# Fixed places for the side work on TensorE and VectorE in a one-core transformer layer

## The chip, the core and the metric

The kernel runs on one core of one Trainium2 chip. The metric is device time in microseconds (us): lower is better. Every time below comes from repeated runs of the kernel or from one profiled execution of it.

## The reference

One layer works on 256 latent tokens and 256 context tokens of width 2048, all in float32. Only the latent stream is returned.

```python
mod_x = split((silu(c) @ w_mod + b_mod), 6)          # shift, scale, gate; shift, scale, gate
h  = rms_norm(x, g_mix) * (1 + mod_x[1]) + mod_x[0]  # and the same for the context tokens
qa, ka, va, qb, kb, vb, rb, lrf, lrb, gate_a, gate_b = split(h @ w_in)
qa, ka = rope(rms_norm(qa)), rope(rms_norm(ka))
o_attn = windowed_attention(qa, ka, va, cka, cva, sink)        # 16 query heads, 4 key heads
o_gla  = latent_gla(qb, kb, vb, gf, gb, context states)        # 4 heads, forward and backward
y_att  = o_attn @ w_attn_o
y_gla  = (rms_norm(o_gla) * silu(rb)) @ w_gla_o
x = x + mod_x[2] * ((sigmoid(gate_a) * y_att + sigmoid(gate_b) * y_gla) @ w_out)
h2 = rms_norm(x, g_ffn) * (1 + mod_x[4]) + mod_x[3]            # the second norm
u  = conv3(h2 @ w_up) ; a, g = split(u)
x = x + mod_x[5] * ((silu(a) * g) @ w_down)
```

## The kernel before

**Products.** Every operand of a large matrix product is written as a sum of a high and a low part in a reduced float32 form, and a product is three matmuls: high by high, low by high, high by low. Weights come in chunks of 256 rows by 512 columns (512 KB). A chunk is loaded by SyncE's DMA queue into one of seven `raw` tiles, ScalarE copies its high part to `whi` (L61) and VectorE subtracts to get the low part `wlo` (L62); there are three pairs of those. `proj_nat` (L165) multiplies a chunk with two token tiles (twelve matmuls of 512 columns: eight with `whi`, L176 and L177, then four with `wlo`, L181) or with four token tiles (24). `proj_T` (L185) makes transposed outputs, and `proj_pair` (L210) the up projection of the FFN, where one matmul takes the high and low part of `h2` side by side (L219, and L223 for the low weights).

**Side work.** At the head of each chunk `tick()` (L133) emits other work between the products: entries put off with `defer(n, ...)`, steps of one generator "beside" (the GLA of a head in `gla_A`, L509, or an attention group in `attend`, L757), and background steps at a rate in `bg_rate`. The background steps are `mod_latent` (L260): the latent tokens' modulation vector `silu(c) @ w_mod` is summed on VectorE, a raw chunk of `w_mod` at a time, by `macc` (two instructions to a chunk, L282 and L284); a finished part goes through a VectorE transpose and sum (`mtr` L288, `mrs` L290) and a small matmul (`pcl`, L294). These raw chunks go through the same seven `raw` tiles and the same queue as the weights.

**What sets the order.** Loads keep the order in which the program writes them (`load`, L66, chains them). On TensorE, VectorE and ScalarE a scheduler at build time sorts the instructions by its own estimates of when they are ready; on the chip each engine then runs its list in that order, and an instruction that waits holds all that stand behind it. Nothing in the program ties a matmul of the side work to a place between the products, nor a `macc` to a place between the `wlo`.

**Stages,** in the order of time: the first norm and the modulation; context and latent projections with the GLA beside them (to about 520 us), keys `KA` and values `VA` of the attention, the attention groups, the `RB` gate of the GLA output (to about 850 us), then the merge: `w_attn_o`, the two gates and `w_gla_o` in turn for four blocks of 512 columns (`mg_evac`, L873, adds the branches into `m` and puts off the transposes `to_T`, L831), `w_out` (to 1285 us), the second norm, the up projection in two halves with the down projection after each, and the store.

**Around the second norm.** `wo_evac` (L893) multiplies by the gate, adds to `x1`, squares on ScalarE, and puts off four transposes (`ptx1`, L903). After the last block come the sum of squares (L914), `rms_scale` (L325), `token_rows` (L339: two scaled identities `dg`, L344, two products `pr`, L345, and a copy `rrow`, L347), and for each of 16 row blocks `affine_split` (L392: VectorE L394, ScalarE L395, VectorE L396).

**Other places that are touched.** `with_gla` (L657) runs `gla_A` at 1.5 steps to a chunk; inside, the cross terms `kf` and `kg` (L610, L611) feed the products `pa` (L617). `gla_o` (L623) emits a head's output products. `ka_evac` (L723) normalises and rotates the keys (`norm_rope`, L700) and puts off their transposes `ptk` (L729). `rb_evac` (L839) makes `sr` (L844) and puts off its transposes. `dn_evac` (L975) is the end of the down projection.

## Time and profile before

| | |
|---|---|
| three runs | 2039.68, 2039.70, 2042.13 us (median 2039.7) |
| profiled execution | 2039.47 us, span 2037.7 us, mean granted TensorE clock 0.991 |
| TensorE busy | 1979.4 us, 97% |
| VectorE busy | 1430.0 us, 70% |
| ScalarE busy | 960.7 us, 47% |
| weight chunks split | 568, `whi` 1059 ns and `wlo` 1226 ns each |
| `macc` on raw `w_mod` | 240, 751 ns each |

The span is what the profile shows; the execution's own time is 1.8 us more. In a row of the timeline stand the start, the time from the first start to the last end, the engine, the line, the operation, the output and inputs, the size, how many instructions of the kind follow one another, and in brackets how long the engine had been idle before and what ended that. In a row of a window stand the stretch, its length, the busy time of TensorE, of its weight loads, of VectorE, ScalarE and GpSimd, then the granted TensorE clock (1.00 is full, 0.50 half), the share of the DMA engines and the rate. The row of a wait says which engine and line waited for what: us in total, times, the longest.

### The profile page before, as it was taken

What the parts mean: (1) busy time and instruction counts of PE and PEld (TensorE: products, weight loads), DVE (VectorE), ACT (ScalarE), POOL (GpSimd) and SP (SyncE); (2) the same over time, 40 slices, a digit from 0 to 9 for tenths busy, and PEclk for the clock granted to TensorE, in tenths of its full rate; (3) what the DMA queues carried; (4) which work ended last, traced back from release to release, by engine and by line L of the source; (5) the groups of instructions that cost most, each with busy time, mean ns of one, the idle gap of its engine ahead of it and who ended that gap; (6) DMA issues with size and microseconds to landing.
All of it is one profiled execution on the core that took longest, in us unless ns stands there. A gap on an engine that the chain in (4) does not pass through costs nothing.

```text
span 2037.7 us, 27395 instructions
## 1 busy us (share of the span) xinstructions
PE 1979.4 (97%) x10384; PEld 1647.3 (81%) x10384; DVE 1430.0 (70%) x2237; ACT 960.7 (47%) x1394; POOL 38.9 (2%) x62
## 2 busy tenths in 40 slices
PE   6999999999999999999999999899999999999998
PEld 4778888888787777787778888788888888888887
DVE  4657577887758888877775455788887555667754
ACT  4323464553345656444334444565555434556532
POOL 0001000001000000000000000000000000000000
PEclk8999999999999999999999999899999999999999
DMA  9977223345544456788886665577776656555563
GB/s 350 364 259 224 91 77 93 93 135 192 172 146 129 124 184 206 263 271 272 273 269 220 237 207 187 193 248 251 261 245 207 212 193 193 188 187 187 193 211 111
DMA packets 214340, 413.54 MB, mean 203 GB/s; under 512 B 12548, under 2 KB 21092, under 8 KB 213184
## 3 DMA queue, kind: packets, MB, share of 16 engines
q1 hardware_dynamic: 212320, 406.89, 60.5%
q0 software_dynamic: 1360, 4.74, 0.8%
q8 instruction: 81, 1.33, 0.3%
q14 instruction: 51, 0.42, 0.1%
q10 hardware_dynamic: 528, 0.17, 0.0%
HBM read 409.63 MB, written 2.11 MB: 202 GB/s over the span
## 4 chain that ended last, share of the span: by engine, by line
PE 78%; DVE 10%; DMA 8%; ACT 2%; issue 2%; DVEq 0%; POOL 0%; ACTq 0%; SPq 0%
PE acc L176 13%; PE acc L177 13%; PE acc L181 13%; PE acc L219 8%; PE accs L219 8%; DMA raw<-in_w_mod 8%; PE acc L223 4%; PE accs L223 4%; PE acc L203 3%; DVE wlo L62 3%; DVE macc L284 3%; PE acc L206 2%; PE pm L245 1%; PE pa L552 1%; ACT whi L61 1%
## 5 line engine op out<-in xcount | busy, mean ns | idle before, releaser
L61 ACT ACTIVATE whi<-raw 128x1024 fp32r<-128x1024 f32 x568 | 600.9, 1059 | 784.7 <-PE acc L177 500.7
L62 DVE TENSOR_TENSOR wlo<-raw,whi 128x1024 fp32r<-128x1024 f32 x568 | 694.1, 1226 | 335.4 <-ACT whi L61 302.6
L284 DVE SCALAR_TENSOR_TENSOR macc<-raw,ccol,macc 128x512 f32<-128x512 f32 x240 | 180.3, 751 | 110.5 <-DMA raw<-in_w_mod 107.0
L219 PE MATMUL acc<-h,whi 128*128 128x512 f32 x704 | 178.6, 396 | 2.2 <-DVE h L396 2.2
L219 PE MATMUL accs<-h,whi 128*128 128x512 f32 x704 | 176.3, 392 | 0.0
L219 PEld LDWEIGHTS acc<-h,whi 128*128 128x128 f32 x704 | 127.8, 191 | 25.6 <-DVE h L396 2.5
L219 PEld LDWEIGHTS accs<-h,whi 128*128 128x128 f32 x704 | 126.6, 189 | 22.6
L176 PE MATMUL acc<-whi,h00hi 128*128 128x512 f32 x352 | 141.2, 401 | 1.5 <-DVE kb L412 0.6
L176 PE MATMUL acc<-whi,h01hi 128*128 128x512 f32 x352 | 139.8, 397 | 0.0
L177 PE MATMUL acc<-whi,h00lo 128*128 128x512 f32 x352 | 139.8, 397 | 0.0
L177 PE MATMUL acc<-whi,h01lo 128*128 128x512 f32 x352 | 137.7, 391 | 0.0
L177 PE MATMUL acc<-whi,al 128*128 128x512 f32 x352 | 137.1, 389 | 0.0
L176 PE MATMUL acc<-whi,ah 128*128 128x512 f32 x352 | 137.0, 389 | 0.0
L223 PEld LDWEIGHTS acc<-h,wlo 128*128 128x128 f32 x704 | 97.0, 192 | 7.1
L223 PEld LDWEIGHTS accs<-h,wlo 128*128 128x128 f32 x704 | 96.0, 190 | 6.9
L223 PE MATMUL acc<-h,wlo 128*128 128x256 f32 x704 | 99.1, 284 | 0.0
L181 PE MATMUL acc<-wlo,h00hi 128*128 128x512 f32 x352 | 98.0, 394 | 0.2 <-DVE wlo L62 0.2
L223 PE MATMUL accs<-h,wlo 128*128 128x256 f32 x704 | 98.2, 282 | 0.0
L181 PE MATMUL acc<-wlo,h01hi 128*128 128x512 f32 x352 | 97.0, 393 | 0.0
L181 PE MATMUL acc<-wlo,ah 128*128 128x512 f32 x352 | 94.4, 389 | 0.0
L176 PEld LDWEIGHTS acc<-whi,h00hi 128*128 128x128 f32 x352 | 66.9, 190 | 15.6 <-ACT kb L410 0.7
L181 PEld LDWEIGHTS acc<-wlo,h00hi 128*128 128x128 f32 x352 | 65.8, 189 | 14.4 <-DVE wlo L62 1.0
(375 smaller groups left out, 3461.5 us busy)
## 6 DMA issues: line engine op xcount, KB each, us to landing
raw<-in_w_in SPq DMA_DIRECT2D x208, 512.0 KB, 4.1
raw<-in_w_up SPq DMA_DIRECT2D x176, 512.0 KB, 3.6
raw<-in_w_mod SPq DMA_DIRECT2D x128, 512.0 KB, 4.0
raw<-in_w_down SPq DMA_DIRECT2D x88, 512.0 KB, 3.7
mraw<-in_w_mod SPq DMA_DIRECT2D x32, 1024.0 KB, 11.9
raw<-in_w_attn_o SPq DMA_DIRECT2D x32, 512.0 KB, 4.5
raw<-in_w_gla_o SPq DMA_DIRECT2D x32, 512.0 KB, 4.7
raw<-in_w_out SPq DMA_DIRECT2D x32, 512.0 KB, 3.6
```

Source lines behind the costliest of these rows:

```text
L61: S.activation(hi, src, AF.Copy)
L62: V.tensor_tensor(lo, src, hi.bitcast(F32), op=ALU.subtract)
L176: PE.matmul(banks[i], ahi, hi[:, k, :], start=(kt == kts[0]), stop=False)
L177: PE.matmul(banks[i], alo, hi[:, k, :], start=False, stop=False)
L181: PE.matmul(banks[i], l(kt)[0], lo[:, k, :], start=False, stop=(kt == kts[-1]))
L203: PE.matmul(o, w_, ahi, start=(kt == kts[0] and b == 0 and part == 0), stop=(kt == kts[-1] and part == 1), skip_group_check=True)
L206: PE.matmul(o, w_, alo, start=False, stop=False, skip_group_check=True)
L219: PE.matmul(banks[f], hi[:, k, f * P:(f + 1) * P], pair(k0 + k), start=(k0 + k == kts[0]), stop=False, skip_group_check=True)
L223: PE.matmul(banks[f][:, 0:T], lo[:, k, f * P:(f + 1) * P], pair(k0 + k)[:, 0, :], start=False, stop=(k0 + k == kts[-1]), skip_group_check= ...
L245: PE.matmul(a[0][q:q + 32, :], cS[:, kt, :], raw[:, k, :], start=(kt < 4), stop=(kt >= 12))
L284: V.scalar_tensor_tensor(a[0], raw[:, k, :], ccol[:, kt:kt + 1], a[0], op0=ALU.mult, op1=ALU.add)
L552: PE.matmul(pa[:, t, :], k2[:, dt, t * P:(t + 1) * P], q2[:, dt, tq * P:(tq + 1) * P], start=(dt == 0), stop=(dt == 1))
```

## The change

The kernel computes the same. It adds 34 matmuls on TensorE; the other engines run the same instructions in another order.

- `mm` notes the last matmul of the projections; `tick` takes it as a pin, and `mm_b` and `turn_b` (now used by all side work on TensorE) make a side matmul stand behind the product that was emitted last ahead of its tick. A dependency without a semaphore ties only the order on the engine.
- A `macc` step stands behind the last `wlo` that was emitted before it.
- `tick` runs all entries that are due, not only those at the head of the list.
- `gla_A` runs at 1.65 steps to a chunk and yields once more ahead of `pa` from `kf`. The outputs of the last head are put off by a tick.
- The transposes of the keys come after 2, 3, 4, 5 ticks instead of 1, 1, 2, 2, and their `y` tile moves to another set of four buffers; those of `rb` and of the merge after 3 and 4 instead of 1 and 2.
- `by_tile`: in the last block of `w_out` and of the last `w_down`, the last chunk does all six products of the first token tile, then those of the second.
- Around the second norm: the scale is made ready early; TensorE's order is the last transposes, 20 transposes of the identity (`pd1`), the two `pr`, 14 more (`pd2`), the first up product; the first `wlo` of the up projection stands behind the last add to `x1`, the others behind the second pair of `h2` that their chunk needs; the `h2` instructions have a fixed order, and the `macc` of the last modulation part come after them all.
- In the last block of the store, the first tile's add stands ahead of the second tile's multiply.

```diff
 
     def split(hi, lo, src):
         S.activation(hi, src, AF.Copy)
-        V.tensor_tensor(lo, src, hi.bitcast(F32), op=ALU.subtract)
+        return V.tensor_tensor(lo, src, hi.bitcast(F32), op=ALU.subtract).ins
+
+    def in_order(*ins):
+
+        for a, b in zip(ins, ins[1:]):
+            tc.add_manual_dep(b, a.name, mybir.DependencyInfo(
+                mybir.DependencyClass.NoSync, mybir.DependencyReason.DATA), reason="order")
+
+    last, pin = [None], [None]
+
+    def mm(*a, **k):
+
+        r = PE.matmul(*a, **k)
+        last[0] = r.ins
+        return r
+
+    def after(i):
+
+        if pin[0] is not None:
+            tc.add_manual_dep(i.ins, pin[0].name, mybir.DependencyInfo(
+                mybir.DependencyClass.NoSync, mybir.DependencyReason.DATA), reason="place among the products")
+        return i
+
+    def mm_b(*a, **k):
+        return after(PE.matmul(*a, **k))
+
+    def turn_b(*a):
+        return after(PE.transpose(*a))
...
 
     def tick():
 
+        pin[0] = last[0]
         for e in later:
             e[0] -= 1
-        while later and later[0][0] < 0:
-            later.pop(0)[1]()
+        due = [e for e in later if e[0] < 0]
+        later[:] = [e for e in later if e[0] >= 0]
+        for e in due:
+            e[1]()
         if beside:
             beside[2] += beside[1]
             while beside[2] >= 1.0:
...
         while bg_rate[1] >= 1.0 and bg_steps:
             bg_rate[1] -= 1.0
             bg_steps.pop(0)()
+        pin[0] = None
 
...
+    hold, last_lo = [], [None]
...
             hi = wh.tile([P, 2, 512], F32R, name="whi", tag="whi")
             lo = wh.tile([P, 2, 512], F32R, name="wlo", tag="wlo")
             n = src.shape[0] // P
-            split(hi[:, 0:n, :], lo[:, 0:n, :], raw[:, 0:n, :])
+            i = split(hi[:, 0:n, :], lo[:, 0:n, :], raw[:, 0:n, :])
+            if hold:
+                in_order(hold.pop(0), i)
+            last_lo[0] = i
         return hi, lo
 
-    def proj_nat(w, r0, c0, kts, lhs, evac):
+    def proj_nat(w, r0, c0, kts, lhs, evac, by_tile=False):
+
 
...
+            if by_tile and k0 + nk > kts[-1]:
+                for i in range(len(lhs)):
+                    part0(i)
+                    part1(i)
+                    if i:
+                        in_order(end, mms[-4])
+                    end = mms[-1]
+            else:
+                for part in (part0, part1):
+                    for i in range(len(lhs)):
+                        part(i)
...
+    behind = []
...
-                    PE.matmul(banks[f], hi[:, k, f * P:(f + 1) * P], pair(k0 + k),
-                              start=(k0 + k == kts[0]), stop=False, skip_group_check=True)
+                    i = mm(banks[f], hi[:, k, f * P:(f + 1) * P], pair(k0 + k),
+                                  start=(k0 + k == kts[0]), stop=False, skip_group_check=True).ins
+                    if behind:
+                        in_order(behind.pop(), i)
...
-    def mod_latent(parts, put=lambda fn: defer(3, fn)):
+    def mod_latent(parts, put=lambda fn: defer(3, fn), begin=None):
...
                 if kt == 0:
-                    V.tensor_scalar(a[0], raw[:, 0, :], ccol[:, 0:1], None, op0=ALU.mult)
+                    i0 = V.tensor_scalar(a[0], raw[:, 0, :], ccol[:, 0:1], None, op0=ALU.mult).ins
+                    if begin is not None:
+                        in_order(begin, i0)
                 else:
-                    V.scalar_tensor_tensor(a[0], raw[:, k, :], ccol[:, kt:kt + 1], a[0],
-                                           op0=ALU.mult, op1=ALU.add)
+                    i0 = V.scalar_tensor_tensor(a[0], raw[:, k, :], ccol[:, kt:kt + 1], a[0],
+                                                op0=ALU.mult, op1=ALU.add).ins
+                if k == 0:
+                    in_order(last_lo[0], i0)
...
-                    PE.matmul(pc, sel[:, 0:32], rs, start=True, stop=True)
+                    mm_b(pc, sel[:, 0:32], rs, start=True, stop=True)
...
         yield
+        yield
         pa = bank("pa", (P, 2, T), side=True)
         for t in range(2):
             for i, (kk, qq) in enumerate(((kf, q2), (kg, q3))):
                 for dt in range(2):
-                    PE.matmul(pa[:, t, :], kk[:, dt, t * P:(t + 1) * P], qq[:, dt, :],
+                    mm_b(pa[:, t, :], kk[:, dt, t * P:(t + 1) * P], qq[:, dt, :],
                               start=(i == 0 and dt == 0), stop=(i == 1 and dt == 1))
...
-        beside[:] = [gla_A(h, kb, qbt, res), 1.5, 0.0]
+        beside[:] = [gla_A(h, kb, qbt, res), 1.65, 0.0]
...
-        gla_o(h, a, *v)
+        if h < 3:
+            gla_o(h, a, *v)
+    defer(1, lambda: gla_o(3, a, *v))
...
-        z = norm_rope(b, rk if i < 2 else None, i % 2)
+        z = norm_rope(b, rk if i < 2 else None, i % 2, "fa")
...
-                PE.transpose(pt[:, h, :], z[:, h, :], ident)
+                turn_b(pt[:, h, :], z[:, h, :], ident)
...
-        defer(1 + i // 2, turn)
+        defer(2 + i, turn)
...
-            defer(1 + t, lambda: to_T(s_, gh, gl, j, t))
+            defer(3 + t, lambda: to_T(s_, gh, gl, j, t))
...
-            defer(1 + t, lambda: to_T(a2[t], mh, ml, j, t))
+            defer(3 + t, lambda: to_T(a2[t], mh, ml, j, t))
...
+    added, turned = [], []
     for j in range(4):
         def wo_evac(t, b, j=j):
...
-            V.tensor_tensor(x1[t][:, js], x1[t][:, js], y, op=ALU.add)
+            added.append(V.tensor_tensor(x1[t][:, js], x1[t][:, js], y, op=ALU.add).ins)
...
-                    PE.transpose(pt[:, k, :], x1[t][:, j * 512 + k * P:j * 512 + (k + 1) * P], ident)
+                    turned[:] = [turn_b(pt[:, k, :], x1[t][:, j * 512 + k * P:j * 512 + (k + 1) * P],
+                                              ident).ins]
...
-        proj_nat(A["w_out"][0], 0, j * 512, ALL, [tok(mh, ml, 0), tok(mh, ml, 1)], wo_evac)
+        proj_nat(A["w_out"][0], 0, j * 512, ALL, [tok(mh, ml, 0), tok(mh, ml, 1)], wo_evac,
+                 by_tile=(j == 3))
 
 
     flush()
+
+    def keep_busy(n, name):
+
+        pd = bank(name, (P, P), side=True)
+        return [turn_b(pd, ident, ident).ins for _ in range(n)]
+
     s1 = sm.tile([P, 2], F32, name="s1", bufs=1)
     V.tensor_reduce(s1, ss1, op=ALU.add, axis=AX.X)
     r1 = rms_scale(s1, D, [P, 2])
-    V.scalar_tensor_tensor(scale2, scale2, 1.0, gffn, op0=ALU.add, op1=ALU.mult)
-    rrow = token_rows("fb", "rrow", r1)
+    g2 = V.scalar_tensor_tensor(scale2, scale2, 1.0, gffn, op0=ALU.add, op1=ALU.mult).ins
+    in_order(g2, added[0])
+    rows_mm = []
+    busy = keep_busy(20, "pd1")
+    rrow = token_rows("fb", "rrow", r1, rows_mm)
+    in_order(turned[0], *busy, *rows_mm)
+    busy = keep_busy(14, "pd2")
+    in_order(rows_mm[-1], *busy)
+    behind.append(busy[-1])
     h2 = [M(f"h2{i}", [P, 4, 2, T], F32R) for i in range(4)]
+    pairs = []
     for kt in range(KT):
         xk = x1T[kt // 8][:, kt % 8, :]
-        affine_split(h2[kt // 4][:, kt % 4, 0, :], h2[kt // 4][:, kt % 4, 1, :], xk, rrow,
-                     scale2[:, kt:kt + 1], shift2[:, kt:kt + 1])
+        pairs.append(affine_split(h2[kt // 4][:, kt % 4, 0, :], h2[kt // 4][:, kt % 4, 1, :], xk, rrow,
+                                  scale2[:, kt:kt + 1], shift2[:, kt:kt + 1]))
+
+    in_order(pairs[0][0], *[i for kt in range(1, KT) for i in (pairs[kt][0], pairs[kt - 1][1])], pairs[-1][1])
+    hold.extend([added[-1]] + [pairs[2 * c + 1][1] for c in range(1, 8)])
     sums = []
-    bg_steps.extend(mod_latent([(5, gcol2)], sums.append))
+    bg_steps.extend(mod_latent([(5, gcol2)], sums.append, pairs[-1][1]))
     bg_rate[:] = [0.36, 0.0]
...
+        ends = []
         for j in range(4):
...
-                V.tensor_tensor(y, b, gate2[:, js], op=ALU.mult)
+                a_ = V.tensor_tensor(y, b, gate2[:, js], op=ALU.mult).ins
                 if half == 0:
                     V.tensor_tensor(x1[t][:, js], x1[t][:, js], y, op=ALU.add)
                 else:
-                    V.tensor_tensor(y, x1[t][:, js], y, op=ALU.add)
+                    if j == 3:
+                        in_order(*ends, a_)
+                    ends[:] = [V.tensor_tensor(y, x1[t][:, js], y, op=ALU.add).ins]
...
             proj_nat(w_down, blocks[0] * 512, j * 512, list(range(n * 4)), [tok(ah, al, 0), tok(ah, al, 1)],
-                     dn_evac)
+                     dn_evac, by_tile=(half == 1 and j == 3))
```

`token_rows` hands its two products back in the list `mms`, and `affine_split` its two VectorE instructions. All calls of `PE.matmul` and `PE.transpose` in the side work that are not shown become `mm_b` and `turn_b`, and those in the projections `mm`.

How it moves instructions is shown at three places. A number behind a name is that of the tile in the program (a `raw` with a larger number is written later in the program's order, and loaded later). In the changed kernel all projection matmuls stand on line 74 and the side work's on line 89, since these are the new helpers' lines.

**VectorE ahead of the second norm.** `yo` and `x1` are the end of `w_out`, `s1` the sum of squares, `wlo_11009`, `wlo_11038` and `wlo_11023`, `wlo_11045` those of the first up chunks. Before:

```order
L284 SCALAR_TENSOR_TENSOR macc_11032<-raw_11101,ccol_96,macc_11032 128x512
L62 TENSOR_TENSOR wlo_11009<-raw_11006,whi_11008 128x1024
L896 TENSOR_TENSOR yo_10876<-acc_10718,gate1_10304 128x512
L62 TENSOR_TENSOR wlo_11038<-raw_11035,whi_11037 128x1024
L897 TENSOR_TENSOR x1_0_10203<-x1_0_10203,yo_10876 128x512
L896 TENSOR_TENSOR yo_10880<-acc_10719,gate1_10304 128x512
L897 TENSOR_TENSOR x1_1_10204<-x1_1_10204,yo_10880 128x512
L284 SCALAR_TENSOR_TENSOR macc_11032<-raw_11201,ccol_96,macc_11032 128x512 x2
L914 TENSOR_REDUCE s1_10896<-ss1_10209 128x2
```

And with the change:

```order
L62 TENSOR_TENSOR wlo_10861<-raw_10858,whi_10860 128x1024
L964 TENSOR_TENSOR yo_10876<-acc_10718,gate1_10304 128x512
L965 TENSOR_TENSOR x1_0_10203<-x1_0_10203,yo_10876 128x512
L964 TENSOR_TENSOR yo_10880<-acc_10719,gate1_10304 128x512
L965 TENSOR_TENSOR x1_1_10204<-x1_1_10204,yo_10880 128x512
L62 TENSOR_TENSOR wlo_11023<-raw_11020,whi_11022 128x1024
L990 TENSOR_REDUCE s1_10896<-ss1_10209 128x2
```

The pair of `macc` between the last add and the sum is gone, and of the two `wlo` of the up projection that stood ahead of the last add, one now stands behind it and the other after the first four row blocks of `h2`.

**TensorE at the first transposes of the keys,** `ptk`. Each product of the second chunk of `VA` stands there by its operands; `wlo` products end a chunk. Before:

```order
L181 MATMUL acc<-wlo,h00hi 128x512 x4
L181 MATMUL acc<-wlo,h10hi 128x512 x2
L176 MATMUL acc<-whi,h00hi 128x512
L729 MATMUL ptk<-ident,sq 128x128 x4
L177 MATMUL acc<-whi,h00lo 128x512
L176 MATMUL acc<-whi,h10hi 128x512
```

And with the change:

```order
L74 MATMUL acc<-wlo,h00hi 128x512 x4
L74 MATMUL acc<-wlo,h10hi 128x512 x4
L89 MATMUL ptk<-ident,sq 128x128 x4
L74 MATMUL acc<-whi,h00hi 128x512
L74 MATMUL acc<-whi,h00lo 128x512
```

The first transposes stand 37 products after the first of `VA` before, and 48 after it with the change, that is at the end of its second chunk. The second, third and fourth stand 8, 23 and 38 products later than they did.

**VectorE in the merge,** around the evacuation of `w_gla_o`'s second block, whose branches are `m2`. Before:

```order
L62 TENSOR_TENSOR wlo_8233<-raw_8230,whi_8232 128x1024
L875 TENSOR_TENSOR m2_7653<-m2_7653,m1_5374 128x512
L874 TENSOR_TENSOR m2_7654<-acc_8016,m2_7654 128x512
L284 SCALAR_TENSOR_TENSOR macc_8209<-raw_8349,ccol_96,macc_8209 128x512
L62 TENSOR_TENSOR wlo_8276<-raw_8273,whi_8275 128x1024
L875 TENSOR_TENSOR m2_7654<-m2_7654,m1_5375 128x512
```

And with the change:

```order
L62 TENSOR_TENSOR wlo_8233<-raw_8230,whi_8232 128x1024
L942 TENSOR_TENSOR m2_7653<-m2_7653,m1_5374 128x512
L941 TENSOR_TENSOR m2_7654<-acc_8016,m2_7654 128x512
L343 SCALAR_TENSOR_TENSOR macc_8209<-raw_8207,ccol_96,macc_8209 128x512
L62 TENSOR_TENSOR wlo_8269<-raw_8266,whi_8268 128x1024
L942 TENSOR_TENSOR m2_7654<-m2_7654,m1_5375 128x512
```

The `macc` stood there with `raw_8349`, which is loaded behind the `raw_8273` of the `wlo` that follows it; with the change it stands there with `raw_8207`, which is loaded ahead of the `raw_8230` of the first row.

More of the change, by code (lines that the diff above doesn't have):

```diff
@@ L308, in rows_from_cols @@
         pt = bank("pt_" + name, (KT, P), side=True)
-        PE.transpose(pt, col, ident)
+        turn_b(pt, col, ident)
         row = sm.tile([KT, P], F32, name="row", tag="t128", bufs=2)
@@ L344, in token_rows @@
             V.tensor_scalar(dg, ident, cols[:, t:t + 1], None, op0=ALU.mult)
-            PE.matmul(pr[:, t * P:(t + 1) * P], ones[:, 0:P], dg, start=True, stop=True)
+            i = PE.matmul(pr[:, t * P:(t + 1) * P], ones[:, 0:P], dg, start=True, stop=True).ins
+            if mms is not None:
+                mms.append(i)
         r = W2(tag, name, [P, T])
@@ L793, in attend @@
                 for h in range(4):
-                    PE.transpose(pt[:, h, :], sc[h][:, k * P:(k + 1) * P], ident)
+                    turn_b(pt[:, h, :], sc[h][:, k * P:(k + 1) * P], ident)
                 th = W2("fb", "pth", [P, 512], F32R)
@@ L833, in to_T @@
         for k in range(4):
-            PE.transpose(pt[:, k, :], src[:, k * P:(k + 1) * P], ident)
+            turn_b(pt[:, k, :], src[:, k * P:(k + 1) * P], ident)
         q4 = slice((j % 2) * 4, (j % 2) * 4 + 4)
```

55 lines of the change are left out of this document (29 added, 26 removed).

## The prediction

> **What bounds the kernel now.** I read the page first, then the list of TensorE's waits, then the timelines of TensorE and VectorE around the longest of them, and last windows for the granted clock.
>
> ```profile
> PE 1979.4 (97%) x10384; PEld 1647.3 (81%) x10384; DVE 1430.0 (70%) x2237; ACT 960.7 (47%) x1394; POOL 38.9 (2%) x62
> ```
>
> TensorE is the bound, and the change removes no product. What can be won is idle TensorE time and time at half clock. TensorE's waits that the change touches:
>
> ```profile
> PE pr L345 <- DVE dg L344: 9.4, 3, 3.2
> PE pa L617 <- DVE kf L610: 4.5, 4, 1.7
> PE ptk L729 <- DVE sq L718: 3.7, 1, 3.7
> PE pto L834 <- DVE m L875: 3.5, 2, 2.8
> PE ptx L903 <- DVE x L897: 2.9, 2, 2.2
> PE acc L181 <- DVE wlo L62: 2.4, 6, 0.8
> PE acc L219 <- DVE h L396: 2.2, 1, 2.2
> PE pto L834 <- DVE sr L844: 1.4, 1, 1.4
> ```
>
> All end on VectorE. One of the three `pr` waits, 3.2 us, is at the second norm; the other two are in the first and stay. That makes 4.5 + 3.7 + 3.5 + 2.9 + 2.4 + 2.2 + 1.4 + 3.2 = 23.8 us of waits, the most that the change could win apart from the clock and the end. After three of these places the clock falls to half:
>
> ```profile
> 1285.50:1288.50 3.00, 0.63 (x4) 0.42 (x4) 2.96 (x5) 1.05 (x4) 0.00 (x0) 1.00 1.04 384
> 1288.52:1302.17 13.65, 7.80 (x25) 6.39 (x26) 8.46 (x24) 6.41 (x15) 0.00 (x0) 0.50 0.25 83
> 1302.20:1310.00 7.80, 7.80 (x45) 6.79 (x45) 7.62 (x14) 4.54 (x9) 0.00 (x0) 1.00 0.44 134
> 537.60:544.40 6.80, 5.66 (x16) 4.58 (x17) 5.45 (x10) 2.77 (x4) 0.00 (x0) 0.50 0.00 0
> 1022.28:1025.69 3.41, 3.41 (x10) 2.63 (x10) 3.34 (x10) 0.60 (x1) 0.00 (x0) 0.50 0.80 249
> 343.03:346.44 3.41, 1.79 (x8) 1.63 (x9) 2.57 (x4) 3.15 (x6) 0.00 (x0) 1.00 0.00 1
> 346.44:349.85 3.41, 3.41 (x17) 2.89 (x16) 1.70 (x3) 1.09 (x2) 0.00 (x0) 1.00 0.00 0
> ```
>
> A stretch with TensorE busy 0.63 of 3.00 us (21%) is followed by half clock; one with 1.79 of 3.41 (52%) is not.
>
> **The second norm.** TensorE, then VectorE:
>
> ```profile
> 1284.42 1.07 PE L181 MATMUL acc<-wlo,mh 128*128 128x512 f32 x4
> 1293.27 1.19 PE L345 MATMUL pr<-dg,ones 128*128 128x128 f32 x4 [3.17 <-DVE dg L344]
> 1296.65 3.78 PE L219 MATMUL acc<-h,whi 128*128 128x512 f32 x8 [2.18 <-DVE h L396]
> 1318.81 2.00 PE L219 MATMUL acc<-h,whi 128*128 128x512 f32 x8
> 1321.60 2.00 PE L219 MATMUL accs<-h,whi 128*128 128x512 f32 x8
> ...
> 1285.07 0.69 DVE L896 TENSOR_TENSOR yo<-acc,gate 128x512 f32<-128x512 f32 x1
> 1285.71 1.23 DVE L62 TENSOR_TENSOR wlo<-raw,whi 128x1024 fp32r<-128x1024 f32 x1
> 1288.17 0.69 DVE L897 TENSOR_TENSOR x<-x,yo 128x512 f32<-128x512 f32 x1
> 1289.73 1.54 DVE L284 SCALAR_TENSOR_TENSOR macc<-raw,ccol,macc 128x512 f32<-128x512 f32 x2 [0.86 <-DMA raw<-in_w_mod]
> 1291.18 0.15 DVE L914 TENSOR_REDUCE s<-ss 128x2 f32<-128x8 f32 x1
> ```
>
> Four products in 1.07 us are 0.227 us each at full clock (a chunk of twelve is 2.72 us). With the sums tile by tile the first tile's is done four products, 0.9 us, earlier, so its `yo` starts at 1284.2. The four operations follow at 0.6 us without a `wlo` between them and end at 1286.7; the `wlo` that now stands behind ends at 1287.9, and covers ScalarE's square. The sum, without the `macc` pair and its 0.86 us wait for a raw chunk, starts at about 1288.0 instead of 1291.18. From there to the first up product it took 5.47 us, with `pr` at half clock; at full clock 0.6 less: 1292.9 instead of 1296.65, 3.75 us won. The eight chunks of the first up block took 1321.60 - 1296.65 = 24.95 us; at full clock one takes 1321.60 - 1318.81 = 2.79, eight 22.3: another 2.6 us. Together **-6.3 us**. VectorE was busy 7.62 of 7.80 us there, so it has hardly room; I take TensorE's pace, and -2 if the clock falls or VectorE sets it, -7 at most.
>
> The 34 fillers are transposes of the identity. The trace has none here, but has transposes of that size, and they bear on whether fillers hold the clock at all:
>
> ```profile
> 8.46 3.74 PE L373 MATMUL ptx<-ident,x 128*128 128x128 f32 x16
> 12.98 1.53 PE L373 MATMUL ptx<-ident,x 128*128 128x128 f32 x12 [0.24 <-DVE xr L376]
> ```
>
> At the start of the program sixteen take 3.74 us (0.23 each), and twelve right behind take 1.53 (0.12 each, with their end in it): the pace doubled after a stretch in which TensorE had hardly anything but transposes. So they count as work. By 0.115 us each the fillers are 2.3 and 1.6 us. The first twenty lie between the last `ptx` (1287.2) and `pr` (1290.1), 2.9 us; the other fourteen between the end of `pr` (1290.6) and the first up product, 2.3 us. They cost nothing, with 0.6 us of cover; were it gone, up to 1 us. With them and `pr`, TensorE is busy about 4.4 of 5.7 us, 77%, above the 52% at which the clock stood.
>
> The Trainium skill speaks against it: "TensorE: Matmul & The Clock Gate", section "Part 4: PE-mode transpose", says that a transpose does not count as busy for the clock in the same way. The trace disagrees in the first 13 us (0.23 us to 0.12 us a transpose). By that rule the fillers would be useless, and the first rival would hold.
>
> **Keys and values.** TensorE, then VectorE:
>
> ```profile
> 525.19 1.07 PE L181 MATMUL acc<-wlo,h11hi 128*128 128x512 f32 x4
> 538.74 1.11 PE L729 MATMUL ptk<-ident,sq 128*128 128x128 f32 x4 [3.72 <-DVE sq L718]
> ...
> 529.34 1.54 DVE L284 SCALAR_TENSOR_TENSOR macc<-raw,ccol,macc 128x512 f32<-128x512 f32 x2 [2.12 <-DMA raw<-in_w_mod]
> 538.00 0.69 DVE L718 TENSOR_TENSOR sq<-sq,y 128x512 f32<-128x512 f32 x1
> ```
>
> The keys' products end at about 526.1. Their first transposes come 48 products later instead of 37, 10.9 us, so at 537.0. The rotated key was done at 538.7, and 2.12 us before it VectorE had stood for the raw chunk of a `macc`; a `macc` on a chunk loaded earlier has no such wait. I take 0.7 of the 2.1 us as won, since the other `wlo` and `macc` of the stretch stay: done at 538.0, a wait of 1 us in place of 3.7, and none for the later ones (8, 23, 38 products later). A wait that short leaves TensorE above 52%, so the half clock from 538.74 to 544.4 goes too, 5.7 us at half, 2.8 us. Together **-5.5 us** (-2 to -6.5).
>
> **The merge.**
>
> ```profile
> 1018.29 0.66 PE L834 MATMUL pto<-ident,m 128*128 128x128 f32 x4 [0.75 <-DVE m L875]
> 1021.72 0.66 PE L834 MATMUL pto<-ident,m 128*128 128x128 f32 x4 [2.77 <-DVE m L875]
> ...
> 1013.23 1.54 DVE L284 SCALAR_TENSOR_TENSOR macc<-raw,ccol,macc 128x512 f32<-128x512 f32 x2 [1.41 <-DMA raw<-in_w_mod]
> 1020.98 0.68 DVE L875 TENSOR_TENSOR m<-m,m 128x512 f32<-128x512 f32 x1
> ```
>
> `m` is done at 1021.66. The transposes come up to 24 products (5.4 us) later, and VectorE loses the wait for the raw chunk. Both waits, 3.5 us, go, and the 3.41 us at half clock, 1.7: **-5.2** (-2 to -5.2). The same delay takes the 1.4 us of `sr`: **-1.4** (0 to -1.4). Of the 2.4 us of `wlo`, late behind such `macc`, I take **-1.5** (0 to -2.4).
>
> **GLA.** The four waits on `kf`, at most 1.7 us each: its VectorE work comes a chunk (at least 2.72 us) earlier, its products 11 to 15 places (2.5 to 3.4 us) earlier. In a chunk of four token tiles, 24 products or 5.4 us, the first outweighs the second. **-3.5** (0 to -4.5).
>
> **The end.**
>
> ```profile
> 2031.94 1.29 DVE L978 TENSOR_TENSOR yd<-acc,gate 128x512 f32<-128x512 f32 x2 [6.29 <-PE acc L181]
> ```
>
> The first tile's multiply starts 0.9 us earlier and the second's still has to wait for its sum, but three operations follow instead of four: **-0.8** (0 to -0.9).
>
> **What it costs.** A `macc` now stands behind a `wlo`, so its raw tile comes free later, and SyncE's queue, whose next load waits for a tile, holds every load behind it; a late load holds `whi`, `wlo` and the twelve products.
>
> ```profile
> raw<-in_w_in SPq DMA_DIRECT2D x208, 512.0 KB, 4.1
> L61 ACT ACTIVATE whi<-raw 128x1024 fp32r<-128x1024 f32 x568 | 600.9, 1059 | 784.7 <-PE acc L177 500.7
> L62 DVE TENSOR_TENSOR wlo<-raw,whi 128x1024 fp32r<-128x1024 f32 x568 | 694.1, 1226 | 335.4 <-ACT whi L61 302.6
> ```
>
> From issue to `wlo` are 4.1 + 1.06 + 1.23 = 6.4 us; with a tile free three chunks ahead there are 8.2 us, a margin of 1.8. Side products held in place also wait where a sorted list would have put something else. No row prices this: 0 at the least, or less where VectorE has room; upwards the slower rival. Nearer the first, since the margin is positive: **+2.5**.
>
> **The sum.** -6.3 - 5.5 - 5.2 - 1.4 - 1.5 - 3.5 - 0.8 + 2.5 = -21.7 us against the profiled execution's 2039.47: **2017.8 us**. That execution lies 0.2 us under the median, so it stands for the runs.
>
> **The rivals.**
>
> *The clock falls all the same.* For it: the clock fell at 1288.5 although no wait before was over 2.2 us, so short gaps are enough where little stands between them. Against it: the pace of the transposes at the start, and 77% busy where 52% held. Then `pr` and the up block lose 0.6 + 2.6 = 3.2 us again: 2021.0; with the half clocks of keys and merge, 2.8 + 1.7, it is 2025.5. Chance 0.15. (The rule of the Trainium skill, "TensorE: Matmul & The Clock Gate", "Part 4: PE-mode transpose", would give the 2021.0.)
>
> *The waits only move.* The change ties side work to its place without making VectorE faster; where VectorE is full (5.45 of 6.80 us at the keys, 3.34 of 3.41 in the merge), a later transpose finds its input late again. For it: the full windows; against: 5.4 us of delay for waits of 2.8 us at most. Keys, merge, `sr` and `wlo` would then win nothing: 2017.8 + 5.5 + 5.2 + 1.4 + 1.5 = 2031.4. Chance 0.12.
>
> *Slower: late tiles in the ring of seven.* If `macc` holds its tile so long that a load starts less than 6.4 us ahead of its use, each pair of chunks with a `macc` loses some of TensorE's time. From 850 to 1280 us are 430 / 5.44 = 79 pairs. At 0.4 us each that is 32 us: 2050. It decides from 21.7 / 79 = 0.28 us a pair. For it: the DMA engines are busy 0.80 of the time at 1022; against: the margin of 1.8 us. Chance 0.08.
>
> **How the numbers follow.** The forecast has 0.65, between 2010 and 2024 by its bounds. Down to 2010 the range leaves out little, since all terms at their best and no cost give 2039.47 - 27.9 = 2011.6; up to 2031 it takes in the first rival and half of the second: 0.62 + 0.14 + 0.06 = 0.82. A difference under 0.2%, 4.1 us, cannot be told from none. Faster than 2035.6: the forecast, the first rival and nearly all of the second, 0.65 + 0.15 + 0.10 = 0.90. The same: 0.04, from the second and a mild third. Slower: 0.06, the third.
>
> **What would show it.** Right: the sum of squares within 2 us of the last add to `x1` begun, full clock throughout 1285 to 1316, the first up block 6 us earlier against the last `w_out` product; no wait over 1.5 us at `ptk`, none at `pto`; no `macc` with a wait for its raw chunk on VectorE from 520 to 1285. Wrong: half clock at the fillers (first rival), the same waits on `sq` and `m` under the new lines (second), or many new waits of `whi` on the DMA of a weight chunk (third).

## The result: 2017.35 us, 1.1% faster

The changed kernel takes 2017.35 us (median of four runs, 2015.56 to 2021.99), the kernel before 2039.69 (four runs, 2035.98 to 2042.13). The ratio is 0.9891, 95% interval 0.9876 to 0.9907. The forecast was 2017.8 us. The profiled execution took 2015.56 us, its span is 2013.8, 23.9 less than the 2037.7 before.

The page and the list of TensorE's waits, in the profile after. Rows of a wait: who waited for whom, us in total, times, the longest.

```profile
PE 1971.1 (98%) x10418; PEld 1642.8 (82%) x10418; DVE 1432.6 (71%) x2237; ACT 960.8 (48%) x1394; POOL 43.9 (2%) x62
...
PE pr L406 <- DVE dg L405: 6.4, 3, 3.2
...
PE pa L86 <- DVE q L636: 3.9, 4, 2.0
PE pa L86 <- DVE kf L674: 2.8, 4, 1.0
PE ptx L89 <- issue: 1.8, 1, 1.8
...
PE pt_cb L137 <- DMA rows<-in_conv_b: 1.2, 1, 1.2
PE pto L89 <- DVE sr L911: 1.1, 1, 1.1
PE ptx L89 <- DVE x L965: 1.0, 2, 0.7
```

The waits of `ptk` on `sq` (3.7 us), of `pto` on `m` (3.5) and of products on a late `wlo` (2.4) are gone. `kf` is down from 4.5 to 2.8, `sr` only from 1.4 to 1.1, and there are new waits of 1.8 us at `ptx` and of 1.2 at `pt_cb`. VectorE's `macc`, before and after (instructions, busy time and mean of one, then VectorE's idle time ahead of them and what ended it):

```profile
L284 DVE SCALAR_TENSOR_TENSOR macc<-raw,ccol,macc 128x512 f32<-128x512 f32 x240 | 180.3, 751 | 110.5 <-DMA raw<-in_w_mod 107.0
L343 DVE SCALAR_TENSOR_TENSOR macc<-raw,ccol,macc 128x512 f32<-128x512 f32 x240 | 180.1, 750 | 3.8
```

The 107.0 us that it waited for raw chunks are gone.

The second norm, in TensorE's and VectorE's timelines after:

```profile
1268.00 0.61 PE L74 MATMUL acc<-wlo,mh 128*128 128x512 f32 x2
1270.22 0.63 PE L89 MATMUL ptx<-ident,x 128*128 128x128 f32 x4 [0.73 <-DVE x L965]
1270.68 2.35 PE L89 MATMUL pd<-ident 128*128 128x128 f32 x20
1273.21 0.68 PE L406 MATMUL pr<-dg,ones 128*128 128x128 f32 x4 [0.18 <-DVE dg L405]
1273.73 1.69 PE L89 MATMUL pd<-ident 128*128 128x128 f32 x14
1275.95 2.11 PE L74 MATMUL acc<-h,whi 128*128 128x512 f32 x8 [0.53 <-DVE h L459]
1298.40 2.00 PE L74 MATMUL accs<-h,whi 128*128 128x512 f32 x8
...
1269.38 0.69 DVE L965 TENSOR_TENSOR x<-x,yo 128x512 f32<-128x512 f32 x1
1269.99 1.22 DVE L62 TENSOR_TENSOR wlo<-raw,whi 128x1024 fp32r<-128x1024 f32 x1
1271.12 0.15 DVE L990 TENSOR_REDUCE s<-ss 128x2 f32<-128x8 f32 x1
```

From the start of the last product of `w_out` to the first up product it is now 1275.95 - 1268.23 = 7.72 us; before it was 1296.65 - 1285.10 = 11.55 (the last products of the rows start 0.227 and three times 0.227 us after the row). The first up block takes 1298.40 - 1275.95 = 22.45 us, before 24.95. The clock, in windows of the profile after (length, busy time of TensorE, its weight loads, VectorE, ScalarE, GpSimd, then the granted clock):

```profile
1268.30:1271.70 3.40, 2.43 (x20) 1.93 (x19) 3.12 (x6) 3.36 (x8) 0.00 (x0) 1.00 0.00 0
1271.70:1275.10 3.40, 3.22 (x30) 3.00 (x28) 1.88 (x8) 0.84 (x4) 0.00 (x0) 1.00 0.56 154
1275.10:1290.00 14.90, 14.37 (x83) 12.46 (x82) 14.72 (x29) 10.82 (x18) 0.00 (x0) 1.00 0.45 125
```

It stays full, with TensorE busy 71% and more.

**Where the time went.** Both kernels run the same 8864 projection products, all but 78 of them at the same place in the order (the 78 stand in five short stretches where neighbours change places). So a stretch from one product to another, counted from the first, can be laid beside the same stretch of the other kernel. From the starts in the two timelines:

| Stretch, by the count of products | before | after | difference |
|---|---|---|---|
| from the start of the profile to the 841st product | 193.52 | 189.81 | -3.7 |
| latent projections ahead of the GLA | 56.95 | 58.65 | +1.7 |
| GLA, with `KA` | 275.62 | 275.94 | +0.3 |
| `VA` and the start of the attention, with the keys' transposes | 53.55 | 46.72 | -6.8 |
| attention and most of `RB` | 238.84 | 240.50 | +1.7 |
| the end of `RB` | 35.93 | 33.96 | -2.0 |
| merge, two blocks to about 1000 us | 157.36 | 152.63 | -4.7 |
| merge, the four chunks with the waits on `m` | 17.51 | 12.12 | -5.4 |
| the rest of the merge and `w_out`, but for the next row | 243.87 | 243.97 | +0.1 |
| `w_out`, where its second block starts | 11.72 | 13.70 | +2.0 |
| second norm and first up block | 47.91 | 41.57 | -6.3 |
| from there to the last product | 699.19 | 699.22 | 0.0 |
| from the start of the last product to the end | 5.73 | 5.01 | -0.7 |

The first row is not the change's: its first 48 products took 22.08 us before and 19.33 after, and 22.0 to 22.7 in all eleven other profiles taken for this study, whose program is the same there. Stretches at half clock fell differently: one of 3.4 us after, three before.

### The profile page after: what moved, and what is told of

Read it like the earlier page. It is cut to its first block, busy times and chain, and to the rows that moved or that the text cites. A ratio compares the mean times of both kernels' runs of the same rounds, so it can differ in the third digit from the quotient of the medians.

```text
span 2013.8 us, 27449 instructions
## 1 busy us (share of the span) xinstructions
PE 1971.1 (98%) x10418; PEld 1642.8 (82%) x10418; DVE 1432.6 (71%) x2237; ACT 960.8 (48%) x1394; POOL 43.9 (2%) x62
## 4 chain that ended last, share of the span: by engine, by line
PE 60%; issue 16%; DVE 0%; POOL 0%; DMA 0%; ACT 0%; POOLq 0%
PE acc L74 47%; PE accs L74 12%; PE pto L89 0%; POOL att L764 0%; DMA glan<-in_gla_norm 0%; PE ptx L89 0%; POOL att L762 0%; PE pcl L86 0%; DVE yd L1072 0%; DVE yd L1066 0%; DVE yo L964 0%; DVE wlo L62 0%; DVE og L910 0%; DVE x L965 0%; PE pr L406 0%
## 5 line engine op out<-in xcount | busy, mean ns | idle before, releaser
L74 PEld LDWEIGHTS accs<-h,whi 128*128 128x128 f32 x704 | 126.6, 189 | 22.7
L74 PEld LDWEIGHTS acc<-whi,ah 128*128 128x128 f32 x352 | 66.1, 188 | 13.7
```

The source lines that it names most:

```text
L74: r = PE.matmul(*a, **k)
```

## The experiments

In each, the stretches of the table are compared as well as the times; between single profiles of kernels that do the same there, they agree within 0.1 us in most of the merge and behind it. All edits but that of the eighth are to the changed kernel.

### Without the fillers

```diff
-    busy = keep_busy(20, "pd1")
+    busy = []
...
-    busy = keep_busy(14, "pd2")
-    in_order(rows_mm[-1], *busy)
-    behind.append(busy[-1])
+    behind.append(rows_mm[-1])
```

> The changed kernel without the 34 filler transposes; all else as it is. Theory (the fillers hold the clock): TensorE is then busy about 0.9 + 0.5 of the 7.8 us between the last product of w_out and the first up product, the granted clock falls to half and the first up block takes some 25 us again instead of 22.3: 2017.4 + 0.6 + 2.6 = 2020.6. Rival (earlier sums and the order of VectorE did it, the fillers are idle weight): the clock stays full and the time is within 1 us of 2017.4.

2022.33 us (2021.36 to 2023.00), ratio to before 0.9915 (0.9901 to 0.9930). TensorE's timeline and windows without the fillers:

```profile
1277.30 0.68 PE L406 MATMUL pr<-dg,ones 128*128 128x128 f32 x4 [2.36 <-DVE dg L405]
1280.04 3.78 PE L74 MATMUL acc<-h,whi 128*128 128x512 f32 x8 [2.05 <-DVE h L459]
...
1271.31:1274.72 3.41, 2.43 (x15) 1.66 (x13) 3.26 (x5) 2.43 (x5) 0.00 (x0) 1.00 0.00 0
1274.73:1278.13 3.40, 0.89 (x6) 0.52 (x4) 1.95 (x9) 1.36 (x6) 0.00 (x0) 1.00 0.48 134
1278.15:1284.95 6.80, 4.91 (x15) 4.18 (x16) 5.27 (x11) 3.27 (x7) 0.00 (x0) 0.50 0.11 16
```

After a stretch with TensorE busy 0.89 of 3.40 us (26%) the clock is half for 6.8 us. The stretch of the second norm takes 43.81 us instead of 41.57. So the fillers hold the clock, worth 2.2 us, and cost nothing: from the last product of `w_out` to the first up product it is 7.71 us without them, 7.72 with them. The two profiled executions lie 6.3 us apart; most of the rest is at the start of the program and at about 247 us, where the program is the same: 22.10 against 19.33 and 59.87 against 58.65.

### The macc free of its place

```diff
-                if k == 0:
-                    in_order(last_lo[0], i0)
```

> The changed kernel with each macc free of its place behind a wlo, so that the scheduler sorts it as before. Theory (a macc that waits for its raw chunk at the head of VectorE's list made wlo, m and the keys late): the macc's waits for raw chunks come back (some 100 us in all on VectorE, 107.0 before), the 4.9 us won from 943 to 998 us are lost again, part of the 6.8 at the keys too, and the 1.8 us wait for the gate at the start of w_out's second block goes: 2017.4 + 4.9 + 2 - 1.8 = 2022.5. Rival (the later transposes did it alone): within 2 us of 2017.4 and no new TensorE wait in that stretch.

2035.77 us (ten runs, 2030.90 to 2039.08), ratio 0.9977 (0.9968 to 0.9986): 18.4 us of the gain of 22.3 are gone. Its waits, of VectorE and of TensorE:

```profile
DVE macc L343 <- DMA raw<-in_w_mod: 99.4, 55, 5.3
...
PE acc L74 <- DVE wlo L62: 5.0, 6, 1.9
...
PE acc L74 <- DVE v3l L62: 2.6, 1, 2.6
...
PE ptk L89 <- DVE sq L783: 2.2, 1, 2.2
```

The waits for raw chunks are back, 99.4 us, and with them late `wlo` and keys, although the transposes stayed late. Against the changed kernel it loses 3.4 us in the GLA, 3.9 at the keys, 8.0 in the two blocks of the merge (2.0 and 6.0), 1.6 in the next four chunks, and 3.8 at the start, which is not the edit's. The wait for the gate at `w_out` stayed (13.40 us), against the expectation.

### The transposes at their old ticks

The keys alone, then the merge alone, then both together.

```diff
-        defer(2 + i, turn)
+        defer(1 + i // 2, turn)
```

> The changed kernel with the keys' transposes after 1, 1, 2, 2 ticks again. Theory (the delay removes the wait): ptk waits about 2 to 3 us again, with half clock behind it: +3 to +6, 2020.4 to 2023.4. Rival (VectorE without the wait for the raw chunk was enough): a ptk wait under 1 us, within 1 us of 2017.4.

2019.26 us (2018.51 to 2020.93), ratio 0.9902 (0.9887 to 0.9917). TensorE has no wait at `ptk`, and the keys' stretch takes 46.82 us (46.72 with the delay). The intervals of the two ratios overlap; of the 3.9 us between the profiled executions, 2.7 lie at the start (22.08 against 19.33).

```diff
-            defer(3 + t, lambda: to_T(s_, gh, gl, j, t))
+            defer(1 + t, lambda: to_T(s_, gh, gl, j, t))
...
-            defer(3 + t, lambda: to_T(a2[t], mh, ml, j, t))
+            defer(1 + t, lambda: to_T(a2[t], mh, ml, j, t))
```

> The changed kernel with the transposes of rb and of the merge after 1 and 2 ticks again. Theory (the delay removes the waits on sr and m): waits of 1.4 and up to 3.5 us come back, with 1.7 for half clock: 2017.4 + 1.4 + 3.5 + 1.7 = 2024. Rival (the macc's place did it): waits under 1 us in all, 2017.4 to 2018.4.

2017.75 us (2017.57 to 2018.70), ratio 0.9895 (0.9878 to 0.9911). No wait on `m`; the two merge stretches take 152.36 and 12.15 us (152.63 and 12.12); the wait on `sr` is 1.1 us with either. And the start of `w_out`'s second block takes 11.72 us, as before the change, instead of 13.70.

> The changed kernel with all transposes at their old ticks: keys after 1, 1, 2, 2, rb and merge after 1 and 2. Theory (with the macc in its place the delays earn nothing, and the longer ones make the gate of w_out 2 us late): 2017.4 - 2 = 2015.4, with 11.7 us for the first four chunks of w_out's second block instead of 13.7. Rival (each alone was covered by the other): 2020 or more.

2019.15 us (2016.90 to 2020.76), ratio 0.9887 (0.9868 to 0.9906): in the total neither the 2 us less that were expected nor clearly the 3 more of the rival. Keys 46.83, merge 152.36 and 12.15, `w_out` 11.72. So the stretches say that the delays earn nothing where the `macc` is in its place, and cost the 2.0 us at `w_out`; in the profiled execution the start of the program hides it (22.65 against 19.33 us, and 59.32 against 58.65 ahead of the GLA).

What makes `w_out` wait is an 8 KB transfer. The evacuation of its blocks multiplies by `gate`, a row that GpSimd's queue writes out to `dgate` (8 KB) and reads back for all partitions, behind the transposes. GpSimd's and TensorE's timelines with the delays, and the transfers' medians from issue to landing:

```profile
1188.47 0.52 POOL L374 DMA_DIRECT2D dgate<-row  x1 [394.18 <-ACT row L372]
1192.88 0.55 POOL L376 DMA_DIRECT2D gate<-dgate  x1 [3.90 <-PE acc L74]
1200.40 0.69 DVE L964 TENSOR_TENSOR yo<-acc,gate 128x512 f32<-128x512 f32 x1 [3.23 <-DMA gate<-dgate]
1202.93 0.63 PE L89 MATMUL ptx<-ident,x 128*128 128x128 f32 x4 [1.77 <-issue]
...
gate<-dgate POOLq DMA_DIRECT2D x1, 1024.0 KB, 7.4
dgate<-row POOLq DMA_DIRECT2D x1, 8.0 KB, 3.8
```

And with the merge's transposes at their old ticks:

```profile
gate<-dgate POOLq DMA_DIRECT2D x1, 1024.0 KB, 6.9
dgate<-row POOLq DMA_DIRECT2D x1, 8.0 KB, 1.9
```

`dgate` lands after 3.7 to 4.2 us in the eight kernels with the merge's later transposes and after 1.8 to 1.9 in the five without, before among them; it is issued 0.3 us later there, counted from the first product of `w_out`. The profile puts the 1.77 us at `ptx` down to "issue", but `yo` is the instruction that waited, for `gate`. Why the small transfer takes twice as long there was not tried; that it meets a weight load is an assumption.

### The GLA's own edits undone

```diff
-        beside[:] = [gla_A(h, kb, qbt, res), 1.65, 0.0]
+        beside[:] = [gla_A(h, kb, qbt, res), 1.5, 0.0]
...
-        yield
         yield
...
-        if h < 3:
-            gla_o(h, a, *v)
-    defer(1, lambda: gla_o(3, a, *v))
+        gla_o(h, a, *v)
```

> The changed kernel with the GLA's own edits undone: 1.5 steps to a chunk, one yield ahead of pa, the last head's output products not put off; all places still held. Theory (those edits earned nothing, as GLA took 253.79 us with the change and 253.47 before): within 1.5 us of 2017.4. Rival (without them the waits on kf return, and the place of the macc alone made GLA worse): +3 to +5, 2020.4 to 2022.4.

2020.67 us (2017.74 to 2023.52), ratio 0.9895 (0.9875 to 0.9915). The waits on `kf` in this kernel:

```profile
PE pa L86 <- DVE kf L674: 4.1, 4, 1.1
```

They are 1.3 us longer than with the edits, and yet the GLA, counted to the middle of `KA`, takes 253.22 us against 253.79. The edits earn nothing. The 3.3 us more lie at the start (22.66), at a half clock of 3.4 us ahead of the GLA, and in `w_out` (15.57 against 13.70, with another at 1208).

### TensorE's places free

```diff
     def after(i):
-        if pin[0] is not None:
+        if False:
```

> The changed kernel with the side products on TensorE free of their places (mm_b and turn_b pin nothing); the macc's place, the delays and the order at the second norm stay. Theory (the scheduler puts them in nearly the same places anyhow, so that VectorE's order alone matters): within 1 us of 2017.4. Rival (TensorE's places carry part of the gain at the keys and in the merge): +3 or more, 2020.4.

2018.84 us (2017.06 to 2021.59), ratio 0.9887 (0.9868 to 0.9907). No stretch from the GLA to the end differs from the changed kernel's by more than 0.5 us. TensorE's order hardly changes either: apart from lines renumbered, the two lists differ where the last head's output products stand and in one `pcl`. The places on TensorE earn nothing here, since the scheduler puts the side products where their inputs come, and VectorE's order decides that.

### The macc's place alone

The kernel before, with the three edits that tie a `macc`:

```diff
-            split(hi[:, 0:n, :], lo[:, 0:n, :], raw[:, 0:n, :])
+            last_lo[0] = split(hi[:, 0:n, :], lo[:, 0:n, :], raw[:, 0:n, :])
...
+                if k == 0:
+                    in_order(last_lo[0], i0)
```

> The kernel before with one thing changed: each macc stands behind the last wlo ahead of it in the program. Theory (the macc's place carries the keys and the merge): their gains come, about 6 at the keys and 5 in each of the two parts of the merge, no TensorE wait on m over 1 us; the second norm is near to before, as its macc pair still stands ahead: 2040 - 14 = 2026. Rival (it needs the delays or TensorE's places beside it): 2033 or more.

2021.70 us (2021.40 to 2024.07), ratio 0.9900 (0.9879 to 0.9920): 19.2 us of the gain. The keys take 47.24 us, the merge 152.23 and 12.11, as with the whole change, with no wait at `ptk` and none on `m`. The second norm takes 46.73, 1.2 less than before. Its rows there:

```profile
1275.57 0.16 DVE L923 TENSOR_REDUCE s<-ss 128x2 f32<-128x8 f32 x1 [0.79 <-ACT yo L907]
...
1281.15 3.78 PE L226 MATMUL acc<-h,whi 128*128 128x512 f32 x8 [2.18 <-DVE h L405]
1306.14 2.00 PE L226 MATMUL accs<-h,whi 128*128 128x512 f32 x8
```

The `macc` pair ahead of the sum is gone without the fixed order, and the first up block still takes 24.99 us, at half clock.

### The macc's place and the second norm alone

The delays, the GLA's edits and TensorE's places undone together (the diffs above). The small edits to `tick`, to the buffers of the keys' `y` and to the two ends (tile by tile) stay in.

> The changed kernel with all but two of its parts undone: the macc's place and the order around the second norm (with the order tile by tile at the two ends) stay; transposes at their old ticks, GLA as before, nothing pinned on TensorE by tick. Theory (these two parts carry the whole gain and add up): macc alone 2021.7, less 5.2 at the second norm (46.73 - 41.57 us from its first product) and 0.8 at the end: 2015.7, the gate of w_out in time. Rival (the rest earns something together): 2019 or more.

2017.86 us (2012.79 to 2018.38), ratio 0.9886 (0.9865 to 0.9908), the same as the whole change. Keys 46.85, merge 152.36 and 12.15, `w_out` 11.72, second norm 41.59. So the two parts, with the small edits that stay, carry the gain; the `macc`'s place alone gave 19.2 us of it without them. That this version, without the 2 us at `w_out`, is faster than the change does not show in the total.

### A ring of six

```diff
-    wr = pool(name="wr", bufs=7)
+    wr = pool(name="wr", bufs=6)
```

> The changed kernel with six raw tiles instead of seven. It prices the ring. Theory (a macc in its place leaves a margin of 1.8 us or more; a chunk is 2.72): at most 3 us more than the changed kernel, in the stretches where every other load is a macc's. Rival (the ring is at its limit already, which is the cost that was put at 2.5): 10 us or more, with whi waiting for loads of weight chunks all over the stretch with macc.

One run: 2021.08 us. The start (22.64 us) and a half clock ahead of the GLA (59.81) make up 4.5 us of the difference to the profile after; where every other pair of chunks has a `macc`, nothing is lost. Its window over the merge's start:

```profile
841.00:1010.00 169.00, 169.00 (x756) 138.94 (x755) 136.23 (x168) 72.32 (x74) 0.00 (x0) 1.00 0.86 288
```

TensorE is never idle, and all merge stretches equal those with seven tiles; from the first up block to the last product it takes 0.3 us more. In the merge the ring was not at its limit.

### Not tile by tile

```diff
-        proj_nat(A["w_out"][0], 0, j * 512, ALL, [tok(mh, ml, 0), tok(mh, ml, 1)], wo_evac,
-                 by_tile=(j == 3))
+        proj_nat(A["w_out"][0], 0, j * 512, ALL, [tok(mh, ml, 0), tok(mh, ml, 1)], wo_evac)
...
-                     dn_evac, by_tile=(half == 1 and j == 3))
+                     dn_evac)
```

> The changed kernel without the order tile by tile in the last chunks of w_out and of the last w_down. Theory (the first tile's sum four products earlier takes 0.9 us off both chains): the first up block 0.5 to 0.9 us later against the last product of w_out, the end 0.6 to 0.9 us later. Rival (VectorE's order alone sets both): no difference over 0.2 us.

One run: 2020.94 us. The second norm takes 42.37 us instead of 41.57, and from the start of the last product to the end it is 5.84 instead of 5.01. Both are 0.8 us.

## Why the prediction was right

The time was right within 0.5 us, and that it came so near is luck. The terms were not all right; their errors cancel. The profile's 23.9 us hold 3.7 from the program's start that the change did not make, so 20.2 stand against the 21.7 forecast. What was right is that waits of TensorE on a late VectorE, and the half clock behind them, were what could be won; what was wrong in two of the three large terms is which edit wins them.

| Term | forecast | measured | |
|---|---|---|---|
| second norm | -6.3 | -6.3 | right, part by part |
| keys | -5.5 | -6.8 | size near, cause wrong |
| waits on `m` and half clock | -5.2 | -5.4 | size right, cause wrong |
| `sr` | -1.4 | -0.3 | wrong |
| late `wlo` | -1.5 | -4.7 | too small |
| GLA | -3.5 | +0.3 | wrong |
| the end | -0.8 | -0.7 | right |
| costs | +2.5 | +3.7 | size near, place wrong |

**Second norm: right.** Against the last product of `w_out` the sum starts 3.2 us earlier (forecast 3.2) and the first up product 3.83 (3.75); the up block is 2.5 us shorter (2.6). The parts were told apart: the place of the `macc` gives 1.2 us, the fillers 2.2, tile by tile 0.8, which leaves 6.3 - 4.2 = 2.1 for the fixed order on VectorE, if the parts add up; that order was not taken out by itself. The fillers are free, as argued from the waits that cover them. The first rival, that the clock falls all the same, is refuted by the windows at full clock; without fillers it does fall.

**Keys: the step that failed is "I take 0.7 of the 2.1 us as won".** The prediction put 2.0 us on the delay of 11 products and 0.7 on the `macc` without its wait. With the old ticks the keys' stretch is the same (46.82 us), and with the `macc` free but the delay in place 3.9 us are lost. The place of the `macc` made VectorE early enough by itself, and no wait was left; the 1 us of wait that the forecast left is most of the difference to the -5.5.

**Merge: the step that failed is "The transposes come up to 24 products (5.4 us) later".** With them at their old ticks there is no wait on `m`. The place of the `macc` did all of it.

**Late `wlo`: mis-sized.** The 2.4 us are the waits in TensorE's list. Windows over the same products, before and after:

```profile
952.10:1011.80 59.70, 57.24 (x244) 44.44 (x243) 43.00 (x52) 22.57 (x23) 0.00 (x0) 1.00 0.82 271
```

```profile
943.40:998.20 54.80, 54.80 (x243) 45.12 (x242) 42.92 (x53) 22.20 (x23) 0.00 (x0) 1.00 0.87 291
```

The stretch was 4.9 us longer than TensorE's work, as the changed kernel does it in 54.80 without a gap. Half of that was idle time, and half is a busy time of 57.24 for the same products: a product of 512 columns is shown as busy for 0.39 us while the next starts 0.227 us after it, so the first 0.16 us of every wait hide under the product before, and shorter ones hide altogether. The list of waits leaves them out, and the 23.8 us of waits that the prediction called the most that could be won were no bound. The time that a stretch has beyond its products, at 0.227 us each, would have shown it.

**GLA: wrong.** The step "the first outweighs the second" is not what failed, since the waits on `kf` did fall (4.5 us before, 4.1 with the `macc`'s place, 2.8 with the edits as well). But the stretch did not get shorter. With `KA`, TensorE's idle time in it fell from 6.4 to 5.4 us, as a new wait of 0.5 us on `v3l` took part of the gain, while its busy time for the same matmuls rose from 269.2 to 270.6 us; where that comes from is open.

**`sr`: wrong.** Its wait moved to another block (from 854 to 798 us) and is 1.1 us, with delays or without. It stands there in every kernel with the `macc` in its place (0.8 to 1.6 us); with the `macc` free and the transposes late there is none. So the `macc`'s place brings it, and the sign "none at `pto`" did not come. Of the 1.7 us more in the attention's stretch it is the larger part; the rest is open.

**Costs.** The ring of tiles, which the prediction named, costs nothing, even with one tile less. What did cost was not seen: the transfer of the gate, 2.0 us, which the later transposes bring about, and 1.7 us ahead of the GLA. There, every kernel with the `macc` in its place takes 58.2 to 59.9 us against 56.95 before and 57.21 with the `macc` free. It is idle time: TensorE is busy 55.5 us in that stretch before and after. The wait of `pa` on `q` is 1.9 to 2.0 us in those eleven kernels against 1.5 before, and `pt_cb`, a transpose of the convolution's bias, waits 0.3 to 1.4 us for the transfer of that bias, 1.2 in the changed kernel and not at all before. In seven of the eleven a half clock of 3.4 us at about 248 us comes on top. Why the `macc`'s place makes these two late is open.

**Rivals.** "The waits only move" is refuted for keys and merge and true for `sr`. "Slower: late tiles in the ring of seven" is refuted by the time itself and by the ring of six.

## What to carry to other kernels

An instruction that waits for a transfer at the head of a busy engine's list delays everything behind it, and where that engine feeds the bound one, the wait shows under other names there (`sq`, `m`, `wlo`); look for the wait on the feeding engine, and give the instruction a place late enough that its data have landed, before moving the consumers. When several edits are made together, take them out one at a time: here one dependency and one fixed stretch gave nearly all of the gain; the order tile by tile gave 0.8 us at the end, the keys' delays, the GLA's edits and TensorE's places nothing, and the merge's delays cost 2 us. Short idle stretches ahead of a dense stage cost twice where the clock falls, and a few matmuls of no use in them can be free.

## What the runs showed of the hardware

The clock follows how busy TensorE was over a short stretch, not its longest gap. In each of the thirteen profiles all changes of the clock lie whole steps of 3.413 us apart. Cut each profile into these steps, from 12 us to 6 us before the end: of those at full clock, every one with TensorE busy under 44% was followed by half clock, none with 49% or more was, and between these both occur. At one fall the longest gap within the step was 0.7 us (41% busy, at the start of the program in the kernel with the `macc`'s place alone), while after a step with a gap of 1.9 us (46%, at 245 us with TensorE's places free) the clock stayed. So it also matters whether an idle stretch falls into one step or is parted between two: after the wait of 1.9 to 2.0 us ahead of the GLA the clock fell in seven of eleven kernels, where its step was 42 to 45% busy, and stayed in the other four (46% in one; 57% or more where two steps shared the wait). The 1.5 us of the kernel before left the step 56% busy there, and the clock stayed. The changed kernel is near the edge where it waits for the gate: that step is 48% busy and the clock stayed; with the GLA's edits undone it is 39%, and the clock fell. Stretches at half clock were 3.4, 6.8, 10.2 and 13.65 us long. The Trainium skill, "TensorE: Matmul & The Clock Gate", section "Part 1: The HAM clock gate", gives a free-running window of 3413 ns; the lengths are one to four of these, so the trace agrees.

Transposes count as work for it. That was argued from the pace at the program's start; the 34 transposes of the identity take 2.35 and 1.69 us here, and with them the clock stays full, without them it falls. The same page of the Trainium skill, "Part 4: PE-mode transpose", says otherwise; the measurement decides, for transposes as this kernel makes them.

An 8 KB transfer on GpSimd's queue landed after 1.8 to 1.9 us in the five kernels without the merge's later transposes and after 3.7 to 4.2 in the eight with them, with no value between.
